# Sixteen attention chunks on TensorE: a planner's order, and an order that is written down

## The chip, the cores and the metric

The kernel runs on one core of a Trainium2 chip. The core has five engines that work side by side, each through its own queue and in the order of that queue: TensorE (PE) does matmuls, VectorE (DVE) and ScalarE (ACT) do element-wise work, GpSimd (POOL) does some more of it, and SyncE (SP) issues DMA transfers. Semaphores tell one engine that another is done. The metric is the time of one execution on the device in microseconds (us); lower is better.

## The reference

The program is a trunk of two layers on 1024 tokens of width 1024. The part that matters here is the first head group of the first layer: sliding-window attention over chunks of 64 tokens, eight query heads, two key heads, each of width 64, a window of the own chunk and the two before, and one learned "sink" logit for each head:

```python
scores = jnp.einsum('bnqhgd,bnkhd->bnhgqk', qc, kb).astype(jnp.float32) * (d ** -0.5)
m = jnp.maximum(jnp.max(scores, axis=-1, keepdims=True), sink_logit)
p = jnp.exp(scores - m)
denom = jnp.sum(p, axis=-1, keepdims=True) + jnp.exp(sink_logit - m)
p = (p / denom).astype(v.dtype)
out = jnp.einsum('bnhgqk,bnkhd->bnqhgd', p, vb)
```

Beside it the same layer has retention heads and gates, `y = concat(ya * silu(ag), yb * silu(bg)) @ w_out`, and every layer ends with a cross-attention into 256 memory tokens, whose keys are `memn @ wkv`. The second layer is a gated convolution.

## The kernel before

All activations lie transposed, width on the 128 partitions and tokens along the free dimension. Every fp32 operand is split into a high and a low part in a format with fewer bits, and a product is three matmuls, high-high, low-high and high-low (`mm3`, lines 210 to 216). `split` makes the two parts: ScalarE copies (line 230), VectorE subtracts (line 231).

A *projection* (`dense`, line 218) multiplies one weight tile of 128 output rows with all tokens: two halves of 512 tokens, each 8 x 3 = 24 matmuls of 512 columns, then a scaling by VectorE (`scaled`, line 303). A *key tile* (one step of `keys_out`, line 849) makes 128 rows of the memory's keys: 24 matmuls of 256 columns, a split, and two stores to DRAM. Its input is the normalised memory, which `mem_norm` has stored to DRAM and `mem_parts` loads back (line 845). The weights of both arrive through `Weights`: a raw tile is loaded by SyncE (line 86, two buffers), copied by ScalarE (line 97) and subtracted by VectorE (line 98) into one of three pages, in the fixed order in which they are used.

`even_layer` (line 522) first makes keys, values and queries of the window attention, then goes through sixteen chunks. One chunk (`window_chunk`, line 370) does, in this order:

- split its queries (line 382), twelve score matmuls into two PSUM buffers (line 391; they use 64 of the 128 rows, so that two run side by side);
- the softmax: maxima (VectorE, line 394), the shift (lines 397 and 398), exponentials with sums (ScalarE, lines 400 and 403), then VectorE's sum with the sink, reciprocal and scaling (lines 404 to 407) into one of two buffers, `Pe` for even and `Po` for odd chunks;
- eight transposes on TensorE (line 421; four in the first two chunks) and their split into `Th` and `Tl`;
- six values matmuls (three in the first two chunks), and two copies that put the result where the queries were (line 432).

Behind each chunk the loop of lines 548 to 553 traces one piece of other work: one of the six gates' projections (at chunks 1, 3, 6, 8, 11 and 13) or one of the eight key tiles (at chunks 0, 2, 4, 5, 7, 9, 10 and 12). Behind the loop stand the SiLU of the gates (line 555), the product with the attention's result (line 558) and the retention heads with their own projections.

The order in which the program is traced is not the order in which the engines run it. A planner walks through all instructions with estimated durations and appends to each engine's queue whatever is ready first, earlier traced work going ahead. Only where the program asks for it is the order fixed: `issue_after(ins)` makes every instruction that is traced inside the block, and that runs on the engine of `ins`, stand behind `ins` in the queue. In the loop before, nothing is asked for.

Of the kernel before, what the change touches and what calls it, by code (L numbers as in the profile page):

```python
# [22 lines left out]
P = 128  # L23
# [9 lines left out]
EVEN_GATES = (1, 3, 6, 8, 11, 13)  # L33
# [126 lines left out]
class Trunk:  # L160
# [209 lines left out]
    def window_chunk(self, n, Q, Kh, Kl, V, Pt):  # L370
        nc = self.nc
        nk = min(n + 1, 3) * CH
        k0 = max(n - 2, 0) * CH
        odd = n % 2
        p0 = 256 - nk if odd else 0
        cols = slice(p0, p0 + nk)
        Q = Q[n // 8][:, :, (n % 8) * CH : (n % 8) * CH + CH]
        Pn = Pt[odd]

        qh = self.buf("k", "qh", (P, 256), F32R)  # L380
        ql = self.buf("k", "ql", (P, 256), F32R)
        self.split(qh.rearrange("p (j t) -> p j t", j=4), ql.rearrange("p (j t) -> p j t", j=4), Q)
        mx, nm, sm, es = (self.small(k) for k in ("mx", "nm", "sm", "es"))
        sc = [self.ps("sc") for _ in range(2)]
        rows = (slice(0, 64), slice(64, P))
        keys = slice(k0, k0 + nk)
        for jp in range(2):
            j = slice(jp * P, jp * P + P)
            for i, (a, b) in enumerate(((qh, Kh), (qh, Kl), (ql, Kh))):
                for g, r in enumerate(rows):  # L390
                    nc.tensor.matmul(sc[g][:, jp * 256 : jp * 256 + nk], a[r, j], b[r, keys],  # L391
                                     start=i == 0, stop=i == 2)
        for g, ps in enumerate(sc):
            nc.vector.tensor_reduce(mx[:, 2 * g : 2 * g + 2],
                                    ps.rearrange("p (a b) -> p a b", a=2)[:, :, :nk],
                                    AX.X, ALU.max)
        nc.vector.scalar_tensor_tensor(nm, mx, -0.125, self.nsink, ALU.mult, ALU.min)
        nc.vector.tensor_tensor(es, self.sink, nm, op=ALU.add)
        for c in range(4):
            nc.scalar.activation(Pn[:, c, cols], sc[c // 2][:, (c % 2) * 256 : (c % 2) * 256 + nk],  # L400
                                 AF.Exp, bias=nm[:, c : c + 1], scale=0.125,
                                 accum_out=sm[:, c : c + 1])
        nc.scalar.activation(es, es, AF.Exp)
        nc.vector.tensor_tensor(sm, sm, es, op=ALU.add)
        nc.vector.reciprocal(sm, sm)
        for c in range(4):
            nc.vector.tensor_scalar(Pn[:, c, cols], Pn[:, c, cols], sm[:, c : c + 1], None,
                                    ALU.mult)
        Th = self.buf("T", "Th", (P, 2, H), F32R)
        Tl = self.buf("T", "Tl", (P, 2, H), F32R)  # L410
        if n == 0:
            kks = [(0, 0, 64)]
        elif n == 1:
            kks = [(1, 0, P)]
        else:
            b = (n - 3) // 2 if odd else (n - 2) // 2
            kks = [(0, b, P), (1, b + 1, P)]
        for kk, _, rows in kks:
            ps = self.ps("a")
            for c in range(4):  # L420
                nc.tensor.transpose(ps[:rows, c * P : c * P + P],  # L421
                                    Pn[:, c, kk * P : kk * P + rows], self.ident)
            self.split(Th[:rows, kk, :], Tl[:rows, kk, :], ps[:rows, :])
        ps = self.ps("a")
        for i, (kk, b, rows) in enumerate(kks):
            v = slice(b * P, b * P + P)
            self.mm3(ps, V[0][:rows, v], V[1][:rows, v], Th[:rows, kk, :], Tl[:rows, kk, :],
                     i == 0, i == len(kks) - 1)
        for g in range(2):
            r = slice(64 * g, 64 * g + 64)  # L430
            o = ps[r, g * 256 : g * 256 + 256].rearrange("p (j t) -> p j t", j=4)
            nc.vector.tensor_copy(Q[r], o)

    def to_tokens(self, vt, name):

        hi = self.buf("v", name + "h", dt=F32R)
        lo = self.buf("v", name + "l", dt=F32R)
        for h in range(2):
            ps = self.ps("a")
            for i in range(4):  # L440
                c = h * H + i * P
                self.nc.tensor.transpose(ps[:, i * P : i * P + P], vt[:, c : c + P], self.ident)
            c = slice(h * H, h * H + H)
            self.split(hi[:, c], lo[:, c], ps)
        return hi, lo
# [76 lines left out]
    def even_layer(self, xs):  # L522


        nc, io = self.nc, self.io
        k = self.buf("r", "ak")
        self.dense(xs, self.scaled(lambda a, b: k[:, a:b]), tags=("d", "d"))
        Kh, Kl = self.buf("v", "Kh", dt=F32R), self.buf("v", "Kl", dt=F32R)
# [3 lines left out]
        V = self.to_tokens(v, "V")  # L532
        Q = [self.buf("e", "Q", (P, 4, H)) for _ in range(2)]
# [4 lines left out]
        Pt = [self.buf("T", "Pe", (P, 4, 256)), self.buf("T", "Po", (P, 4, 256))]  # L538
# [4 lines left out]
        gates = [lambda a, b, j=j: G[a // H][:, j, :] for j in range(4)]  # L543
# [1 line left out]

        ya = self.dp.tile([2, P, 4, H], F32, name="ya")
        keys = self.keys_out(self.mem_parts(0, "r"), 0, "t")
        for n in range(16):
            self.window_chunk(n, Q, Kh, Kl, V, Pt)
            if n in EVEN_GATES:  # L550
                self.dense(xs, self.scaled(gates[EVEN_GATES.index(n)]))
            else:
                next(keys, None)
        for g in G + GB:
            nc.scalar.activation(g, g, AF.Silu)
        self.use_set(LN_EXP)
# [29 lines left out]
        V = next(kv)  # L586
# [560 lines left out]
```

## Time and profile before

| | us |
|---|---|
| timed runs, median of 3 | 1472.85 |
| lowest and highest run | 1469.6 and 3709.59 |
| profiled execution, its own time | 1468.65 |
| profiled execution, span of the trace | 1466.9 |
| TensorE busy in the span | 1437.5 |
| VectorE busy | 882.2 |
| ScalarE busy | 632.2 |

The granted clock of TensorE is 0.996 on the mean. Rows of the timeline give the start of an instruction, its duration and its engine, line, operands and shape. Matmuls overlap, so their durations are longer than the distance between their starts. Rows of groups give the count behind an x, then the busy time, the mean duration in ns and the idle time before. Rows of stretches give, for a stretch of time, the busy time and number of instructions of TensorE's matmuls, its weight loads, VectorE, ScalarE and GpSimd, then the granted clock, the DMA share and the GB/s.

### The profile page before, as it was taken

Reading aid. Unit: us, or ns where it says so; the run is one execution under the profiler, and the core shown is the slowest. Engines: PE = TensorE matmul, PEld = TensorE weight load, DVE = VectorE, ACT = ScalarE, POOL = GpSimd, SP = SyncE. Lnnn points to the kernel's source line nnn. Section 1 sums busy time; section 2 is a strip of 40 time slices with the busy share of each in tenths; the row PEclk is TensorE's granted clock in tenths of the full one; section 3 lists DMA queues with packets and bytes.
Section 4 is the critical chain, followed back from the end, with each engine's and each line's share of the span. In section 5 each row is a group of like instructions: output and inputs, shape, how many; then the busy total and the mean of one; then the engine's idle time right before and its main releaser. Section 6 shows DMA issues by size and latency. Waiting matters only on the chain.

```text
span 1466.9 us, 18556 instructions
## 1 busy us (share of the span) xinstructions
PE 1437.5 (98%) x7128; PEld 1210.0 (82%) x7128; DVE 882.2 (60%) x1317; ACT 632.2 (43%) x1140; POOL 258.5 (18%) x172
## 2 busy tenths in 40 slices
PE   7999999999998999999999999999999999999997
PEld 5888878888887888888887788888888888888996
DVE  7656767677755346447456986655566327446555
ACT  6434553344346234335334633333352325335554
POOL 2300102234211220000113034222220220000221
PEclk9999999999999999999999999999999999999999
DMA  6442223322354421113765121121135532111464
GB/s 218 148 168 58 90 70 101 101 72 59 112 214 152 155 101 44 30 29 126 223 207 180 47 85 60 58 58 58 58 109 192 187 129 72 37 36 39 128 216 149
DMA packets 55080, 160.45 MB, mean 109 GB/s; under 512 B 6736, under 2 KB 17104, under 8 KB 54224
## 3 DMA queue, kind: packets, MB, share of 16 engines
q1 hardware_dynamic: 54992, 159.27, 33.5%
q8 instruction: 56, 0.92, 0.3%
q14 instruction: 32, 0.26, 0.1%
HBM read 127.78 MB, written 27.26 MB: 106 GB/s over the span
## 4 chain that ended last, share of the span: by engine, by line
PE 86%; DVE 6%; DMA 3%; ACT 2%; issue 1%; SPq 0%; POOL 0%; DVEq 0%; ACTq 0%; POOLq 0%
PE psd L214 18%; PE psd L215 18%; PE psd L216 18%; PE pssc L215 5%; PE pssc L216 5%; PE pssc L214 5%; PE psa L215 4%; PE psa L214 4%; PE psa L216 4%; PE pssc L391 1%; DVE wlo L98 1%; DMA wraw<-w_o 1%; PE psa L421 1%; PE psa L931 1%; DMA wraw<-w_o_in 1%
## 5 line engine op out<-in xcount | busy, mean ns | idle before, releaser
L214 PE MATMUL psd<-xh,whi 128*128 128x512 f32 (+2 forms) x1096 | 412.7, 380 | 10.9 <-ACT whi L97 7.5
L215 PE MATMUL psd<-xl,whi 128*128 128x512 f32 (+2 forms) x1096 | 415.0, 380 | 0.0
L216 PE MATMUL psd<-xh,wlo 128*128 128x512 f32 (+2 forms) x1096 | 414.3, 379 | 0.3 <-DVE wlo L98 0.3
L214 PEld LDWEIGHTS psd<-xh,whi 128*128 128x128 f32 x1096 | 205.9, 188 | 48.3 <-ACT whi L97 8.0
L97 ACT CAST whi<-wraw 128x1024 fp32r<-128x1024 f32 (+1 forms) x136 | 141.8, 1045 | 219.5 <-PE psd L215 137.5
L216 PEld LDWEIGHTS psd<-xh,wlo 128*128 128x128 f32 x1096 | 206.1, 188 | 35.4 <-DVE wlo L98 0.6
L215 PEld LDWEIGHTS psd<-xl,whi 128*128 128x128 f32 x1096 | 206.2, 188 | 34.1 <-DVE xl L243 0.3
L98 DVE TENSOR_TENSOR wlo<-wraw,whi 128x1024 fp32r<-128x1024 f32 (+1 forms) x136 | 171.1, 1260 | 71.4 <-ACT whi L97 71.2
L274 POOL TENSOR_TENSOR ssq<-ssq,xold 128x512 f32<-128x512 f32 (+2 forms) x54 | 84.3, 1561 | 621.5 <-ACT xold L272 566.5
L316 DVE TENSOR_TENSOR xnew<-psd,xold 128x512 f32<-128x512 f32 x32 | 21.9, 690 | 97.6 <-PE psd L216 94.2
L126 ACT CAST wf<-ws 128x512 fp32r<-128x512 f32 x64 | 39.2, 621 | 90.4 <-PE pssc L216 27.2
L127 DVE TENSOR_TENSOR wf<-ws,wf 128x512 fp32r<-128x512 f32 x64 | 58.7, 922 | 23.0 <-ACT wf L126 22.6
L272 ACT ACTIVATE xold<-xnew 128x512 f32<-128x512 f32 (+2 forms) x63 | 36.5, 580 | 66.0 <-DVE xnew L316 33.8
L215 PE MATMUL pssc<-T,wf 128*128 128x512 f32 x156 | 61.3, 394 | 2.2 <-DVE T L231 2.2
L230 ACT CAST Th<-psa 128x512 fp32r<-128x512 f32 (+1 forms) x62 | 34.5, 590 | 64.3 <-PE psa L421 34.5
L214 PE MATMUL pssc<-T,wf 128*128 128x512 f32 x156 | 61.2, 393 | 0.8 <-ACT kept L738 0.8
L216 PE MATMUL pssc<-T,wf 128*128 128x512 f32 x156 | 61.0, 392 | 0.0
L231 DVE TENSOR_TENSOR Tl<-psa,Th 128x512 fp32r<-128x512 f32 (+1 forms) x62 | 41.7, 686 | 25.9 <-ACT Th L230 25.8
L109 POOL TENSOR_TENSOR ws<-wraw 128x512 f32<-128x512 f32 x14 | 18.6, 1332 | 205.3 <-DMA wraw<-w_o_in 205.3
L303 DVE TENSOR_TENSOR q<-psd,R 128x512 f32<-128x512 f32 x32 | 22.1, 691 | 53.8 <-PE psd L216 53.8
L214 PE MATMUL psd<-y,whi 128*128 128x512 f32 x128 | 50.0, 391 | 0.0
L215 PE MATMUL psd<-y,whi 128*128 128x512 f32 x128 | 50.0, 391 | 0.0
(339 smaller groups left out, 2888.1 us busy)
## 6 DMA issues: line engine op xcount, KB each, us to landing
wraw<-w_o SPq DMA_DIRECT2D x40, 512.0 KB, 3.7
wraw<-w_o_in SPq DMA_DIRECT2D x37, 512.0 KB, 3.5
wraw<-w_e_in SPq DMA_DIRECT2D x25, 512.0 KB, 3.8
wraw<-w_k SPq DMA_DIRECT2D x16, 512.0 KB, 4.0
mn<-memn SPq DMA_DIRECT2D x16, 512.0 KB, 4.8
wraw<-w_v SPq DMA_DIRECT2D x16, 512.0 KB, 4.5
xold<-x SPq DMA_DIRECT2D x16, 512.0 KB, 4.9
x<-xnew SPq DMA_DIRECT2D x16, 512.0 KB, 2.6
```

The lines of the kernel that those rows point to most:

```text
L97: self.nc.scalar.copy(hi[:, c], raw[:, c])
L98: self.nc.vector.tensor_tensor(lo[:, c], raw[:, c], hi[:, c].bitcast(F32), op=ALU.subtract)
L126: self.nc.scalar.copy(hi, src)
L127: self.nc.vector.tensor_tensor(lo, src, hi.bitcast(F32), op=ALU.subtract)
L214: mm(o, ah, bh, start=first, stop=False, skip_group_check=more)
L215: mm(o, ah, bl, start=False, stop=False, skip_group_check=more)
L216: self.last_mm = mm(o, al, bh, start=False, stop=last, skip_group_check=more)
L230: self.last_cast = self.nc.scalar.copy(hi, src)
L231: return (eng or self.nc.vector).tensor_tensor(lo, src, hi.bitcast(F32), op=ALU.subtract)
L272: nc.scalar.activation(sq, x, AF.Square)
L274: eng.tensor_tensor(self.ssq[:, a:b], self.ssq[:, a:b], sq, op=ALU.add)
L303: return lambda a, b, ps: self.nc.vector.tensor_tensor(out(a, b), ps, self.R[:, a:b], op=ALU.mult)
```

## The change

`window_chunk` becomes a generator with three steps: queries, scores and softmax; transposes and their split; values and their copies. The function `step` runs the next step of a chunk inside `issue_after(self.last_mm.ins)`, so that its matmuls stand behind the last matmul of what was traced before; the gates and key tiles are traced inside such a block, too. `last_mm` is now also set by scores and transposes. The loop traces, for each n from 0 to 16: the gate or key tile of n, the values of chunk n - 1, the scores of chunk n + 1, and the transposes of chunk n. TensorE's order from the first scores to the last values is thereby one row; the order within the other engines remains the planner's, and so does the place of all that is traced behind the loop.

```diff
@@ window_chunk
-                    nc.tensor.matmul(sc[g][:, jp * 256 : jp * 256 + nk], a[r, j], b[r, keys],
-                                     start=i == 0, stop=i == 2)
+                    self.last_mm = nc.tensor.matmul(
+                        sc[g][:, jp * 256 : jp * 256 + nk], a[r, j], b[r, keys],
+                        start=i == 0, stop=i == 2)
...
+        yield
         Th = self.buf("T", "Th", (P, 2, H), F32R)
...
-                nc.tensor.transpose(ps[:rows, c * P : c * P + P],
-                                    Pn[:, c, kk * P : kk * P + rows], self.ident)
+                self.last_mm = nc.tensor.transpose(ps[:rows, c * P : c * P + P],
+                                                   Pn[:, c, kk * P : kk * P + rows], self.ident)
             self.split(Th[:rows, kk, :], Tl[:rows, kk, :], ps[:rows, :])
+        yield
...
             nc.vector.tensor_copy(Q[r], o)
+        yield
@@ even_layer
-        for n in range(16):
-            self.window_chunk(n, Q, Kh, Kl, V, Pt)
-            if n in EVEN_GATES:
-                self.dense(xs, self.scaled(gates[EVEN_GATES.index(n)]))
-            else:
-                next(keys, None)
+        chunks = [self.window_chunk(n, Q, Kh, Kl, V, Pt) for n in range(16)]
+
+        def step(n):
+
+            if 0 <= n < 16:
+                with self.tc.issue_after(self.last_mm.ins):
+                    next(chunks[n])
+
+        step(0)
+        for n in range(17):
+            with self.tc.issue_after(self.last_mm.ins):
+                if n in EVEN_GATES:
+                    self.dense(xs, self.scaled(gates[EVEN_GATES.index(n)]))
+                elif n < 16:
+                    next(keys, None)
+            step(n - 1)
+            step(n + 1)
+            step(n)
```

## The prediction

> **What bounds the kernel now.** I read the page first, then the stretch table cut to the window stage, then the groups of that stage by shape, then the timeline of TensorE and of the two vector engines.
>
> ```profile
> PE 1437.5 (98%) x7128; PEld 1210.0 (82%) x7128; DVE 882.2 (60%) x1317; ACT 632.2 (43%) x1140; POOL 258.5 (18%) x172
> ```
>
> TensorE (PE) is busy for 98% of the span, so time can only be won by making its instructions follow each other faster, and any wait that is put in front of it is lost at once. The stage that the change touches runs from the first scores at 80 us to the last values at 249 us:
>
> ```profile
> 80.00:249.00 169.00, 169.00 (x977) 138.26 (x976) 111.90 (x277) 80.95 (x223) 7.00 (x2) 1.00 0.28 86
> ```
>
> In 169.0 us TensorE does 977 matmuls and is never idle; VectorE (DVE) is busy 111.9 us, ScalarE (ACT) 81.0. So there is no wait here that the change could remove. What it can remove is slowness inside the busy time. The groups say what the 977 are:
>
> ```profile
> L215 PE MATMUL psd<-xl,whi 128*128 128x512 f32 x128 | 50.5, 394 | 0.0
> L215 PE MATMUL psd<-mn,whi 128*128 128x256 f32 x64 | 18.4, 288 | 0.0
> L215 PE MATMUL psa<-Tl,Vh 128*128 128x512 f32 x29 | 11.9, 410 | 0.0
> L391 PE MATMUL pssc<-Kl,qh 64*128 64x192 f32 x56 | 11.6, 287 | 0.0
> L421 PE MATMUL psa<-ident,Po 128*128 128x128 f32 x60 | 8.7, 278 | 0.0
> L98 DVE TENSOR_TENSOR wlo<-wraw,whi 128x1024 fp32r<-128x1024 f32 x16 | 19.5, 1221 | 4.4 <-ACT whi L97 4.4
> ```
>
> Each product is three matmuls (L214 to L216), and the first chunk has smaller shapes under rows of their own. So: 192 matmuls for key tiles, 90 for values, 192 scores (three kinds of 64), 120 transposes (60 of odd chunks, as many of even ones), and the remaining 383 are projections: 288 of the six gates and 95 of the retention's first projections, which the planner has already pulled forward into this stage.
>
> **What TensorE pays for changing its kind of work.** Durations of overlapping matmuls mislead; the distance from start to start is what a matmul costs.
>
> ```profile
> 128.95 0.39 PE L216 MATMUL psd<-xh,wlo 128*128 128x512 f32 x1
> 129.27 0.37 PE L391 MATMUL pssc<-Kh,qh 64*128 64x192 f32 x2
> ...
> 130.13 0.50 PE L214 MATMUL psd<-xh,whi 128*128 128x512 f32 x1
> 130.46 0.40 PE L215 MATMUL psd<-xl,whi 128*128 128x512 f32 x1
> ...
> 130.93 0.40 PE L214 MATMUL psd<-xh,whi 128*128 128x512 f32 x1
> 131.16 1.04 PE L421 MATMUL psa<-ident,Pe 128*128 128x128 f32 x8
> 131.96 0.48 PE L215 MATMUL psd<-xl,whi 128*128 128x512 f32 x1
> 132.27 0.39 PE L216 MATMUL psd<-xh,wlo 128*128 128x512 f32 x1
> ...
> 134.99 0.39 PE L216 MATMUL psd<-xh,wlo 128*128 128x512 f32 x1
> ```
>
> A 512-column matmul behind its like costs 0.227 us (132.27 to 134.99 are twelve of them). The step into scores, which use half of the rows, costs 0.32 (128.95 to 129.27), 0.09 more; all twelve scores of a chunk cost 0.86 (129.27 to 130.13); the first matmul behind them costs 0.33, another 0.10. Eight transposes between projections cost 0.80, 0.10 each. Where scores are cut up, each piece pays again:
>
> ```profile
> 138.68 0.50 PE L214 MATMUL psa<-Th,Vh 128*128 128x512 f32 x1
> 139.11 0.35 PE L391 MATMUL pssc<-Kh,qh 64*128 64x192 f32 x1
> ```
>
> ```profile
> 110.21 1.09 PE L421 MATMUL psa<-ident,Pe 128*128 128x128 f32 x8
> 111.23 0.35 PE L391 MATMUL pssc<-Kl,qh 64*128 64x192 f32 x1
> ```
>
> One values matmul between two pieces of scores takes 0.43 instead of 0.23, and eight transposes that are put into the middle of a score block take 1.02 instead of 0.80.
>
> **The change, part by part.** It removes and adds no instruction that computes, and its edges stand between instructions of one engine, so they bring no semaphore either. *First*, the scores become whole. Priced by the starts above, with 0.120 us for a 256-column matmul:
>
> ```profile
> 122.09 0.28 PE L214 MATMUL psd<-mn,whi 128*128 128x256 f32 x1
> 122.21 0.28 PE L215 MATMUL psd<-mn,whi 128*128 128x256 f32 x1
> ```
>
> 383 x 0.227 + 192 x 0.120 + 90 x 0.227 + 120 x 0.10 + 16 x (0.09 + 0.86 + 0.10) = 86.9 + 23.0 + 20.4 + 12.0 + 16.8 = 159.2 us. The stage takes 169.0, so 9.8 us go. If transposes that follow scores cost 1.02 in the new order too, 15 x 0.22 = 3.3 less goes, 6.5; if the step from scores to transposes pays no 0.10, 1.6 more, 11.4. I take 9.8, since the new order has a projection or key tile behind the transposes, as in the 0.80 case.
>
> *Second*, the freedom to fill waits goes. Now the planner cuts gates and key tiles into pieces and lays them wherever chunk work is not ready. Afterwards everything on TensorE from chunk 0 to chunk 15 stands in one row: filler n, values n-1, scores n+1, transposes n. If transposes n wait, the next whole filler, the next values and scores stand behind them, and only later projections, which are outside the chain, may slip between; these have their weights late, in the last three or four steps. So the price is: how long does softmax n take, from its scores to its normalised rows, against what TensorE has to do meanwhile? Its work in between is transposes n-1, the filler, values n-1 and scores n+1: 0.80 + filler + 6 x 0.227 + 0.95. With a gate as filler (48 x 0.227 = 10.9) this is 14.0 us, with a key tile (24 x 0.120 = 2.9) 6.0. The softmax of chunk 8, whose scores are through when the matmul of 158.63 starts:
>
> ```profile
> 158.63 0.50 PE L214 MATMUL psd<-xh,whi 128*128 128x512 f32 x1
> ```
>
> ```profile
> 158.78 1.02 DVE L394 TENSOR_REDUCE mx<-pssc 128x2 f32<-128x384 f32 x2
> ...
> 161.80 0.68 DVE L231 TENSOR_TENSOR Tl<-psa,Th 128x512 fp32r<-128x512 f32 x1
> ...
> 163.65 1.01 DVE L407 TENSOR_SCALAR Pe<-Pe,sm 128x192 f32<-128x192 f32 x4
> ```
>
> It ends at 163.65 + 1.01 = 164.66, that is 6.0 us after its scores, with the splits of the previous chunk's transposes (Tl) in between, as they will be afterwards. Gates cover that with 8 us to spare. Key tiles cover it with nothing to spare, in eight places (n = 0, 2, 4, 5, 7, 9, 10, 12). A late one is chunk 9, where ScalarE had been sent to the SiLU of the gates and had to reload its table before the exponentials:
>
> ```profile
> 170.93 0.39 PE L214 MATMUL psd<-mn,whi 128*128 128x256 f32 x1
> ```
>
> ```profile
> 175.06 1.28 ACT L400 ACT_TABLE_LOAD   x1 [3.73 <-DVE nm L397]
> ```
>
> ```profile
> 180.40 0.32 DVE L407 TENSOR_SCALAR Po<-Po,sm 128x192 f32<-128x192 f32 x1
> ```
>
> 180.72 - 170.93 = 9.8 us. So one wait costs between 0 and 3.8 us. VectorE has 111.9 / 16 = 7.0 us of work for each chunk, a little less beside a key tile, which has no gate to scale; against 6.0 of TensorE it falls behind by about 1 us where two key tiles follow each other. I take 0.5 us for a lone key tile (n = 2, 4, 7), 1.0 for the second of a pair (5, 10), 2.0 at n = 9 (the table reload of 1.28 and a SiLU in front of it, half hidden under gate 8) and 1.5 at n = 12 (the same for the smaller SiLU): 1.5 + 2.0 + 2.0 + 1.5 = 7.0. Steps 14 and 15 have no key tile left; there the retention's projections fill, as they do now.
>
> *Third*, key tile 0 must be whole before gate 0. Its second half waits for the normalised memory that comes back from DRAM:
>
> ```profile
> L845 SPq DMA_DIRECT2D mn<-memn x4: 320/320/378, 63.5 to 77.7; - x4
> ...
> DMA to landing us min/median/max: 4.2/6.2/7.0
> ```
>
> The last load goes out at 77.7 and lands at 83.9 by the median. Scores 0 and half a key tile take TensorE to 80.4 + 0.9 + 1.4 = 82.7. Now gate 0 covers the rest; afterwards 1.2 us are a wait (0 to 2.0 by the shortest and longest landing).
>
> *At no cost*: the weights. A raw tile and its split (L98, 1.22 us, and as much again for ScalarE's copy) start when the tile three before is done, so even a pair of key steps gives them 12 us. SyncE's queue keeps its loads and the stores of the keys in the same sequence; its DMA share is 0.28. Nothing on GpSimd is moved; its two instructions are 7.0 us. Were a weight late all the same, it would be a wait like those above.
>
> Sum: 1468.65 (the profiled execution) - 9.8 + 7.0 + 1.2 = 1467.0. The timed runs of before lie 1 to 4 us above that execution, so I say 1468. Own range: saving 6.5 to 11.4, waits half to twice as long, and the 1 us of the timed runs: 1462 to 1480.
>
> **The rivals.** *The softmax is in time* (chance 0.25): only the 1.2 us of key tile 0 are left: 1460, timed 1461. For it: VectorE idles 57 us of the stage, and the order of its work is planned anew. Against: 6.0 against 6.0 leaves no room.
>
> *The softmax is late at every key tile* (0.17): as late as chunk 9, eight times 3.8 = 30 us against the 9.8, 1489. For it: fixed order with nothing to lay in between, weight splits of 1.22 us that come free just when a filler ends. Against: only that chunk met a table reload. From 4.9 us for each key tile (29.4 + 9.8, over 8) it is slower than before by 2%.
>
> *Such waits also slow the clock* (0.05). The trace has one place of that kind:
>
> ```profile
> 460.00:464.00 4.00, 1.28 (x6) 0.86 (x5) 1.77 (x2) 1.04 (x1) 1.88 (x1) 1.00 0.44 131
> 464.00:468.00 4.00, 4.00 (x12) 3.13 (x11) 0.21 (x1) 0.11 (x1) 0.00 (x0) 0.57 0.00 0
> ```
>
> After 2.7 us idle out of 4 the clock was 0.57 for the next 4 us, 1.7 us lost. With waits of 3.8 at eight key tiles that is 14 us more: 1503. Waits of 0.5 to 2 us, as in my sum, are shorter than that idle time, and I charge them nothing. [...]
>
> *The order hardly changes* (0.05), because planner and chain agree already: 1469. The rows at 138.68 and 110.21 speak against it.
>
> **How the numbers follow.** Forecast 0.46, rivals as above, 0.02 for a gain that I don't see. From 1455 to 1490 lies all but the clock's rival, the worst part of the late one and the unseen gain, 0.14 together. Two per cent, 29 us, is about what a measurement here tells from no change. The whole switching cost is 11.4 at most, so faster by that has 0.02; slower needs the clock's rival or the end of the late one: 0.07; within: 0.91.
>
> **What would show it.** After: score stretches of twelve, each behind values and followed by eight transposes; their starts 0.9 and 0.8 apart. TensorE idle in the stage of about 8 us, in front of transposes, ended by the normalise of L407, at key steps only, and one of 1.2 ended by a memory load. Clock 1.00 throughout. I am wrong if idle time stands in front of scores or values, if a wait is above 3 us, or if the stages behind differ by more than 5 us.

## The result, and the profile after

The changed kernel takes 1491.1 us (median of four runs, 1488.9 to 1496.9) against 1472.2 for the kernel before on the same chip: a ratio of 1.013, with an interval of 1.0105 to 1.0156. It is slower, by less than 2%. One run of the kernel before took 3710 us; the ratio leaves it out. The profiled execution took 1491.64 us, its span is 1489.9 us, 23.0 more than before, and the mean granted clock is 0.986 (before 0.996). In the changed file the scores are L391, the exponentials L401, the scalings L408, the transposes L423, and the product with the attention's result L574.

The engine row of the page after:

```profile
PE 1445.6 (97%) x7128; PEld 1221.1 (82%) x7128; DVE 871.1 (58%) x1317; ACT 632.3 (42%) x1140; POOL 255.6 (17%) x172
```

TensorE does the same 7128 matmuls in 8.1 us more of busy time, and the rest of the 23 us is idle time. To see where, I cut both traces at the same work: first scores, last values, first matmul of the second half's memory values, last matmul. Stretch rows of before, then of after (columns as before: busy time and count of matmuls, weight loads, VectorE, ScalarE, GpSimd, then clock, DMA share, GB/s):

```profile
80.40:248.50 168.10, 168.10 (x972) 137.71 (x972) 111.53 (x276) 80.54 (x222) 7.00 (x2) 1.00 0.28 85
248.50:423.20 174.70, 174.49 (x865) 146.90 (x864) 124.34 (x153) 65.88 (x119) 60.22 (x36) 1.00 0.33 103
423.20:1456.50 1033.30, 1022.04 (x4987) 868.04 (x4986) 588.18 (x810) 442.39 (x739) 170.21 (x115) 1.00 0.33 107
```

```profile
80.10:257.40 177.30, 169.44 (x957) 143.02 (x957) 109.07 (x273) 80.73 (x222) 5.66 (x2) 0.94 0.26 77
257.40:442.80 185.40, 178.29 (x882) 149.73 (x882) 118.04 (x155) 65.15 (x119) 59.74 (x37) 1.00 0.33 101
442.80:1479.50 1036.70, 1024.66 (x4986) 870.34 (x4985) 585.62 (x810) 443.12 (x739) 169.10 (x115) 0.99 0.33 106
```

The counts differ because the planner now pulls 16 projection matmuls fewer into the stage (363 instead of 379); at 0.227 us that is 3.6 us of work moved from the first row to the second. With that put right, the window stage lost 177.3 - 168.1 + 3.6 = 12.8 us, the stage behind it 185.4 - 174.7 - 3.6 = 7.1, all the rest 3.4. Most of the new clock loss lies in the first row (0.94), the new idle time in the first (7.9) and in the second (7.1, before 0.2).

**The waits in the stage.** Groups of after on TensorE between 80 and 258 us; the last part is the idle time before them and what ended it:

```profile
L391 PE MATMUL pssc<-Kh,qh 64*128 64x192 f32 x56 | 13.1, 323 | 1.5 <-ACT Pe L401 1.1 <-ACT Po L401 0.5
L215 PE MATMUL psa<-Tl,Vh 128*128 128x512 f32 x29 | 12.2, 421 | 2.2 <-DVE Tl L231 2.2
L423 PE MATMUL psa<-ident,Po 128*128 128x128 f32 x60 | 10.0, 318 | 1.5 <-DVE Po L408 1.5
L423 PE MATMUL psa<-ident,Pe 128*128 128x128 f32 x56 | 8.1, 290 | 2.6 <-DVE Pe L408 2.6
```

They sum to 7.8 us. About half (4.1) stands in front of transposes and is ended by the scaling L408. The rest stands in front of scores, ended by the exponentials that still read the score buffers, and in front of one values step, ended by a split.

**The order, and the clock behind a wait.** TensorE's timeline of after around chunk 5, where two key tiles follow each other, and a chunk without a wait:

```profile
132.58 0.35 PE L391 MATMUL pssc<-Kh,qh 64*128 64x192 f32 x1 [0.49 <-ACT Po L401]
132.77 0.27 PE L391 MATMUL pssc<-Kl,qh 64*128 64x192 f32 x1
...
134.03 0.27 PE L391 MATMUL pssc<-Kh,ql 64*128 64x192 f32 x1
135.78 1.94 PE L423 MATMUL psa<-ident,Po 128*128 128x128 f32 x8 [1.48 <-DVE Po L408]
137.37 0.78 PE L214 MATMUL psd<-xh,whi 128*128 128x512 f32 x1
137.94 0.63 PE L215 MATMUL psd<-xl,whi 128*128 128x512 f32 x1
138.37 0.63 PE L216 MATMUL psd<-xh,wlo 128*128 128x512 f32 x1
...
151.89 0.36 PE L391 MATMUL pssc<-Kh,qh 64*128 64x192 f32 x2
...
152.53 0.27 PE L391 MATMUL pssc<-Kh,ql 64*128 64x192 f32 x2
152.74 0.66 PE L423 MATMUL psa<-ident,Pe 128*128 128x128 f32 x4
```

Three things are to be seen. The order is as written: twelve scores, eight transposes, then a gate (the last row counts four transposes, since the window of that view ends inside them). At 151.89 the scores stand as x2, the two halves of the rows side by side, and the transposes start 0.85 us after the first score; at 132.58 they stand as x1, one after the other, and from the first start to the last takes 1.45 us instead of 0.64. And behind the two waits of 0.49 and 1.48 us a 512-column matmul takes 0.43 us from start to start (137.94 to 138.37) instead of 0.227. The stretch rows of after show how long that lasts:

```profile
134.00:142.00 8.00, 6.52 (x22) 5.42 (x22) 4.94 (x19) 3.30 (x12) 0.00 (x0) 0.57 0.20 75
142.00:179.00 37.00, 35.51 (x213) 29.96 (x212) 22.02 (x43) 16.21 (x34) 4.59 (x1) 1.00 0.18 50
179.00:190.00 11.00, 10.26 (x45) 9.15 (x46) 7.87 (x22) 5.79 (x15) 0.00 (x0) 0.53 0.47 164
190.00:196.00 6.00, 3.85 (x25) 3.00 (x23) 4.21 (x12) 3.69 (x13) 0.00 (x0) 1.00 0.41 106
196.00:200.00 4.00, 3.96 (x15) 3.43 (x16) 2.91 (x12) 2.54 (x11) 0.00 (x0) 0.57 0.13 47
```

Three spells at half clock, each with waits of 0.5 to 2.2 us at or just before its start: 8 x 0.43 + 11 x 0.47 + 4 x 0.43 = 10.3 us of clock lost, some of it in time that was idle anyway. The wait of 1.10 us in front of the transposes of chunk 2, at 105.96, has no such spell behind it in this trace.

**The long wait, and GpSimd.** Timelines of GpSimd, VectorE and TensorE of after around chunk 8:

```profile
174.10 1.02 DVE L395 TENSOR_REDUCE mx<-pssc 128x2 f32<-128x384 f32 x2
...
174.22 4.59 POOL L574 TENSOR_TENSOR GA<-GA,Q 128x2048 f32<-128x2048 f32 x1 [98.74 <-ACT qh L230]
...
175.04 4.04 DVE L231 TENSOR_TENSOR ql<-Q,qh 128x256 fp32r<-128x256 f32 x1
...
177.12 0.39 PE L214 MATMUL psa<-Th,Vh 128*128 128x512 f32 x1
...
179.01 0.68 DVE L231 TENSOR_TENSOR Tl<-psa,Th 128x512 fp32r<-128x512 f32 x1
...
179.74 0.80 PE L215 MATMUL psa<-Tl,Vh 128*128 128x512 f32 x1 [2.23 <-DVE Tl L231]
```

The first half of the gates' product runs on GpSimd for 4.59 us. The split `ql` on VectorE, 0.4 us elsewhere, runs beside it for 4.04 and ends when it ends; the splits `Tl` queue behind it, and the values step waits 2.23 us. Before, the same product met `ql` only in its last part: `ql` took 1.80 us, and TensorE did not wait. The second half of the product has a collision of its own, behind the stage:

```profile
262.45 4.62 POOL L574 TENSOR_TENSOR GA<-GA,Q 128x2048 f32<-128x2048 f32 x1 [3.73 <-DVE Q L435]
...
262.65 5.51 DVE L231 TENSOR_TENSOR rot<-bk,rot 128x1024 fp32r<-128x1024 f32 x1 [0.34 <-ACT rot L230]
268.19 0.69 DVE L303 TENSOR_TENSOR bq<-psd,R 128x512 f32<-128x512 f32 x1
...
268.91 0.47 SPq L456 DMA_DIRECT2D swap<-bq  x1
...
275.61 0.66 PE L446 MATMUL psa<-ident,bv 128*128 128x128 f32 x4 [1.65 <-DVE bv L303]
279.58 0.68 PE L214 MATMUL pssc<-rot,rot 128*128 128x512 f32 x2 [2.15 <-ACT rot L230]
```

The retention's rotation split takes 5.51 us instead of 1.23, the scaling of `bq` stands behind it until 268.19, so the DMA that swaps its halves goes out at 268.91, and TensorE waits 1.65 and 2.15 us for what follows from that; a wait of 3.28 us at 327.56 comes later in the same stage. Before, this product stretched the same split (to 4.95 us), but the scaling of `bq` ran ahead of it, at 250.08, and TensorE waited for nothing.

### The profile page after: what moved, and what is told of

It is laid out like the page before. It is cut to its first block, busy times and chain, and to the rows that moved or that the text cites. A ratio compares the mean times of both kernels' runs of the same rounds, so it can differ in the third digit from the quotient of the medians.

```text
span 1489.9 us, 18557 instructions
## 1 busy us (share of the span) xinstructions
PE 1445.6 (97%) x7128; PEld 1221.1 (82%) x7128; DVE 871.1 (58%) x1317; ACT 632.3 (42%) x1140; POOL 255.6 (17%) x172
## 4 chain that ended last, share of the span: by engine, by line
PE 84%; DVE 6%; DMA 4%; ACT 2%; issue 1%; POOL 1%; SPq 0%; DVEq 0%; ACTq 0%; POOLq 0%
PE psd L214 17%; PE psd L215 17%; PE psd L216 17%; PE pssc L215 6%; PE pssc L216 5%; PE pssc L214 5%; PE psa L215 4%; PE psa L214 4%; PE psa L216 4%; DVE wlo L98 1%; PE psa L423 1%; DMA wraw<-w_o 1%; PE psa L947 1%; PE pssc L391 1%; DMA wraw<-w_o_in 1%
## 5 line engine op out<-in xcount | busy, mean ns | idle before, releaser
L98 DVE TENSOR_TENSOR wlo<-wraw,whi 128x1024 fp32r<-128x1024 f32 (+1 forms) x136 | 167.4, 1233 | 76.4 <-ACT whi L97 75.8
```

Source lines behind the costliest of these rows:

```text
L98: self.nc.vector.tensor_tensor(lo[:, c], raw[:, c], hi[:, c].bitcast(F32), op=ALU.subtract)
```

## The experiments

**The product on VectorE.** If the collision is the cause of the 2.23 us and of the waits behind the stage, the product's engine decides, with the written order untouched.

```diff
-            nc.gpsimd.tensor_tensor(G[h], G[h], Q[h], op=ALU.mult)
+            nc.vector.tensor_tensor(G[h], G[h], Q[h], op=ALU.mult)
```

> The changed kernel with one edit: the product of gate and attention result (two instructions of 128x2048) goes from GpSimd to VectorE. Theory A (GpSimd's 4.6 us product slows VectorE beside it: 4.04 us instead of 0.41 for the split of the queries behind chunk 9's maxima, 5.51 instead of 1.22 for the rotated keys later): the wait of 2.2 us before values 8, the clock of 0.66 behind it (some 5 us) and the two waits at 275 to 280 us (3.8 us) go, against 1491 about 1480. Theory B (the softmax's own length against a key tile is the cause, GpSimd is by the way): within 3 us of 1491. Theory C (VectorE's 2 x 2.4 us more lie in the softmax's way): 1491 or more, with new waits before transposes.

Measured: 1484.9 us, 1.0094 of before (1.0071 to 1.0117). Its stretches, stage and behind:

```profile
81.50:255.00 173.50, 166.07 (x958) 140.38 (x957) 107.83 (x274) 81.07 (x222) 1.15 (x1) 0.95 0.26 79
255.00:434.70 179.70, 178.87 (x882) 149.79 (x881) 127.41 (x156) 65.57 (x119) 57.50 (x36) 1.00 0.33 104
```

Behind the stage 5.7 of the 7.1 us are back (185.4 to 179.7). In the stage 3.8 us are back: the values step waits 0.80 instead of 2.23, since the product takes 2.28 us of VectorE itself, and idle time and half clock remain (0.95). So the collision is part of the cause: most of the loss behind the stage, but the smaller part of the loss in it.

**The same in the kernel before**, as a control: if GpSimd's product were simply a bad choice, moving it would make the kernel before faster, too.

```diff
 # in the kernel before
-            nc.gpsimd.tensor_tensor(G[h], G[h], Q[h], op=ALU.mult)
+            nc.vector.tensor_tensor(G[h], G[h], Q[h], op=ALU.mult)
```

> Control: the kernel before, with the product on VectorE. TensorE has no idle time there that the product could have caused, so within 2 us of the kernel before. If it gains 5 us or more, the product was a cost before, too, and what it cost the changed kernel was not brought by the change.

Measured: 1474.5 us, 1.0018 (1.0009 to 1.0028). In the old order the product on GpSimd costs nothing, so what it costs in the new order comes from the change.

**Only the second half of the product**, to part the two collisions.

```diff
-            nc.gpsimd.tensor_tensor(G[h], G[h], Q[h], op=ALU.mult)
+            (nc.vector if h else nc.gpsimd).tensor_tensor(G[h], G[h], Q[h], op=ALU.mult)
```

> The changed kernel with only the second of the two products (behind the last chunk) on VectorE; the first stays on GpSimd beside chunk 9. Theory A, in its two places: the wait of 2.2 us before values 8 and the clock behind it stay, the waits of 1.6, 2.2 and 3.3 us behind the stage go: 1491 less 5 to 6, 1485. If the later waits come from the projections being later: 1490 or more.

Measured: 1487.2 us, 1.0111 (1.0094 to 1.0128). The two rows that matter, the stretch behind the stage and the values step of chunk 8:

```profile
257.60:437.20 179.60, 178.84 (x882) 149.80 (x881) 125.48 (x156) 65.59 (x119) 58.51 (x36) 1.00 0.33 104
```

```profile
180.66 0.50 PE L215 MATMUL psa<-Tl,Vh 128*128 128x512 f32 x1 [2.23 <-DVE Tl L231]
```

The stage behind is repaired by this half alone (5.8 us of span), the 2.23 us in the stage stay. Each half of the product has its own price, as its rows said. The span is 5.1 us shorter than that of the kernel after, the median 3.9; by the timed runs alone the two are not told apart (1.0111 and 1.013, with intervals that overlap), so this rests on the rows.

**No two key tiles in a row.** If VectorE falls behind where two key tiles follow each other, spreading the gates evenly takes those waits away.

```diff
-EVEN_GATES = (1, 3, 6, 8, 11, 13)
+EVEN_GATES = (1, 3, 5, 7, 9, 11)
```

> The changed kernel with the gates at chunks 1, 3, 5, 7, 9 and 11, so that no key tile follows a key tile before chunk 13. Theory B: the waits of 0.5 and 1.5 us at chunk 5 and of 0.7 and 1.5 us at chunk 10, and the half clock behind them (3.3 and 2 us), go; some 8 us less, 1483. The wait at GpSimd's product moves from chunk 9 to the key step behind gate 7 and stays. If a lone key tile is as bad as a pair: within 3 us of 1491.

Measured: 1479.7 us, 1.0051 (1.0033 to 1.0069). Of the stage's waits over 0.4 us one is left, the 1.10 us in front of the transposes of chunk 2, and the stage takes 170.7 us with 32 projection matmuls more than after, 163.4 for the same work. The wait at GpSimd's product, which I expected to stay, is gone as well: `ql` is stretched here too, to 3.44 us, but a gate stands on TensorE beside it. So this edit takes away more than the pairs. And the one wait that is left, which left the clock at 1.00 in the kernel after, is followed by half clock here. Stretches of this experiment:

```profile
104.00:108.00 4.00, 2.90 (x16) 2.76 (x16) 3.91 (x12) 1.73 (x4) 0.00 (x0) 0.64 0.21 70
108.00:112.00 4.00, 4.00 (x11) 3.04 (x11) 2.66 (x10) 2.56 (x11) 0.00 (x0) 0.51 0.46 131
```

and of the kernel after, with the same wait:

```profile
104.00:108.00 4.00, 2.90 (x20) 2.59 (x20) 3.90 (x13) 2.47 (x5) 0.00 (x0) 1.00 0.21 70
```

**Spread gates and the product on VectorE.** The whole written order is kept, both causes are taken away.

```diff
-EVEN_GATES = (1, 3, 6, 8, 11, 13)
+EVEN_GATES = (1, 3, 5, 7, 9, 11)
...
-            nc.gpsimd.tensor_tensor(G[h], G[h], Q[h], op=ALU.mult)
+            nc.vector.tensor_tensor(G[h], G[h], Q[h], op=ALU.mult)
```

> The changed kernel, its chain whole, with both causes taken out in other ways: gates at chunks 1, 3, 5, 7, 9 and 11, and the product on VectorE. If pairs of key tiles and the product are all that is wrong with it: 1491 less 11 (the pairs, as measured alone) less 5 to 6 (the product), 1474 to 1475, still no faster than before; the rest is the wait before transposes 2 and what the key steps lack. If the two overlap: 1479, as without pairs alone.

Measured: 1469.9 us, 0.9986 (0.9974 to 0.9999), better than I expected: the 1.1-us wait was there at 106.4 us, but this time the clock stayed at 1.00. So the written order need not be slow; what made the change slow was what it met. Whether the order itself is worth something this does not show: the interval ends just below 1, the gates stand at other chunks than in the kernel before, and the kernel before was not run with those places.

**The fillers free.** The chunks' steps stay in one row, but gates and key tiles are outside it and may be laid in anywhere, as before.

```diff
-            with self.tc.issue_after(self.last_mm.ins):
-                if n in EVEN_GATES:
-                    self.dense(xs, self.scaled(gates[EVEN_GATES.index(n)]))
-                elif n < 16:
-                    next(keys, None)
+            last = self.last_mm
+            if n in EVEN_GATES:
+                self.dense(xs, self.scaled(gates[EVEN_GATES.index(n)]))
+            elif n < 16:
+                next(keys, None)
+            self.last_mm = last
```

> The changed kernel with gates and key tiles out of the chain: the steps of the chunks stand behind each other as before the edit, but a gate or key tile may go anywhere among them, in pieces. Theory D (what costs is that no filler may go to where the chunk waits; the whole scores, transposes and values are a gain of some 10 us): no idle TensorE and no half clock in the stage, 1460 to 1465. Rival (the pieces of the fillers bring the switching back): 1470 to 1474, as the kernel before. Rival (whole chunk blocks are the cost): 1485 or more.

Measured: 1476.1 us, 1.0031 (1.0017 to 1.0046). The stage came out nearly as expected, at full clock and with 1.98 us of idle time left (1.41 in front of a values step, 0.57 in front of scores); the total didn't:

```profile
80.80:240.20 159.40, 157.42 (x956) 132.64 (x956) 108.99 (x273) 80.67 (x222) 5.67 (x2) 1.00 0.29 86
```

It does the work of the kernel after in 17.9 us less, at full clock. What I had missed is that the collision behind the stage is there again, with waits of 1.64, 2.16 and 3.2 us at 258, 262 and 310 us.

**Fillers free and the product on VectorE**, the two together:

```diff
-            with self.tc.issue_after(self.last_mm.ins):
-                if n in EVEN_GATES:
...
+            last = self.last_mm
+            if n in EVEN_GATES:
...
-            nc.gpsimd.tensor_tensor(G[h], G[h], Q[h], op=ALU.mult)
+            nc.vector.tensor_tensor(G[h], G[h], Q[h], op=ALU.mult)
```

> Both edits on the changed kernel: fillers out of the chain, and the product on VectorE. If the two losses are separate (fillers held back: the stage; GpSimd's product: chunk 9 and the rotations behind the stage), the stage stays as with free fillers alone, 159 us, or 2 less, and the waits of 7.0 us behind it go: 1476 less 7 to 9, 1467 to 1469, some 4 us faster than the kernel before. If the waits behind the stage come from the projections being done later, not from the product: 1474 or more.

Measured: 1467.6 us, 0.9966 (0.9952 to 0.9980), faster than both kernels by a little.

```profile
80.70:237.80 157.10, 157.10 (x956) 132.36 (x956) 107.89 (x274) 80.62 (x222) 1.10 (x1) 1.00 0.29 87
237.80:417.40 179.60, 178.89 (x882) 149.83 (x882) 125.55 (x156) 65.56 (x119) 58.65 (x36) 1.00 0.33 104
```

This is the change without its waits: no idle time in the stage, clock 1.00, the same 363 projections. The kernel before would take 168.1 - 3.6 = 164.5 us for this work, so the saving in switching is 7.4 us. **With spread gates as well**, on top of this edit:

```diff
-EVEN_GATES = (1, 3, 6, 8, 11, 13)
+EVEN_GATES = (1, 3, 5, 7, 9, 11)
```

> Free fillers and the product on VectorE as before, with the gates at chunks 1, 3, 5, 7, 9 and 11 too. With free fillers no wait is left in the stage, so the place of the gates should be worth nothing: 1466 to 1469. If pairs still cost something that the fillers' pieces only hide: 1462 to 1465.

Measured: 1466.6 us, 0.9971 (0.9959 to 0.9984): the same. Where the fillers are free, it doesn't matter at which chunk they are traced.

**Without the scalings.** Which of the stage's waits are VectorE's time for the end of the softmax?

```diff
-        nc.vector.tensor_tensor(sm, sm, es, op=ALU.add)
-        nc.vector.reciprocal(sm, sm)
-        for c in range(4):
-            nc.vector.tensor_scalar(Pn[:, c, cols], Pn[:, c, cols], sm[:, c : c + 1], None,
-                                    ALU.mult)
```

> The changed kernel without the end of the softmax: the sum with the sink, the reciprocal and the four scalings of each chunk are left out (the exponentials go to the transposes unscaled), which takes some 1.6 us out of the softmax's length and of VectorE's work for each chunk. Theory B: the waits before transposes 2, 5, 10 and 12 and the half clock behind them go, the one at GpSimd's product stays: 1478 to 1483. Theory A alone: 1489 or more.

Measured: 1488.7 us, 1.012 (1.0101 to 1.0139). The stage gave back 8.3 us (169.0), and no transposes wait any more; 2.23 us in front of the values step and 0.7 to 0.9 in front of scores are left. The total missed my expectation. The waits behind the stage are other ones but sum to the same 7.1 us (3.86 and 3.23), and the clock, which had stayed at 1.00 behind them in the kernel after, was 0.57 from 270 to 274 us and from 321 to 325 us; that stretch is 2.4 us longer than after, and the first scores come 1.2 us later. I had counted neither, and the scalings have nothing to do with the collision there.

**Busy while it waits.** The half clock was so far only seen beside the waits. To measure its own price I left TensorE's order and what it waits for as they are, and put matmuls whose results are thrown away in front of the waiting steps, so that the array is busy while it would wait.

```diff
+            for _ in range(6 if n in (2, 5, 10) and kk == 0 else 0):
+                nc.tensor.matmul(ps, Kh[:, :P], Kh[:, :H], start=True, stop=True)
...
+        for _ in range(9 if n == 8 else 0):
+            nc.tensor.matmul(ps, Kh[:, :P], Kh[:, :H], start=True, stop=True)
```

> The changed kernel, its order untouched, with idle matmuls in four of its waits: six 512-column matmuls (1.4 us) in front of the transposes of chunks 2, 5 and 10, and nine (2.0 us) in front of the values of chunk 8; they write into the PSUM tile that the next instructions overwrite. Theory E (what the waits cost is mostly the half clock that follows them, 10.2 us in the stage, and TensorE at work keeps the clock up): the waits end at the same times, the clock stays at 1.00 and 6 to 10 us go, 1481 to 1485. Theory F (the clock falls for another reason, or the waits themselves are the cost): 1490 to 1494, since the matmuls only fill time or make the waits longer.

Measured: 1489.5 us, 1.0121 (1.0104 to 1.0137), no gain in the total. Stretches of the stage, then of two waits behind it:

```profile
80.80:251.80 171.00, 168.58 (x985) 141.75 (x985) 109.25 (x273) 80.67 (x222) 5.80 (x2) 0.99 0.27 79
275.00:280.00 5.00, 5.00 (x19) 4.14 (x18) 4.41 (x6) 2.76 (x6) 1.28 (x1) 0.66 0.14 27
325.00:330.00 5.00, 5.00 (x25) 4.11 (x25) 4.71 (x8) 3.81 (x9) 1.70 (x1) 0.86 0.01 3
```

The stage is 6.3 us shorter (171.0 against 177.3) although it does the 27 idle matmuls as well, and the clock is 0.99 instead of 0.94: as the half-clock theory says. But behind it the waits of 1.46 and 2.16 us, which had left the clock at 1.00 in the kernel after, now came with 0.66 in the 5 us after them, and the one of 3.2 us with 0.86. From 439.7 us on, in work that no edit touches, it also took 4.4 us longer than the kernel after, with a wait of 3.52 us at 827.11 where that has 1.90. Its profiled execution, 1492.96 us, is the highest of its runs. To keep that apart, the same **with the product on VectorE**, where nothing waits behind the stage; it is to be compared with the first experiment.

```diff
+            for _ in range(6 if n in (2, 5, 9) and kk == 0 else 0):
+                nc.tensor.matmul(ps, Kh[:, :P], Kh[:, :H], start=True, stop=True)
...
+        for _ in range(4 if n == 8 else 0):
+            nc.tensor.matmul(ps, Kh[:, :P], Kh[:, :H], start=True, stop=True)
...
-            nc.gpsimd.tensor_tensor(G[h], G[h], Q[h], op=ALU.mult)
+            nc.vector.tensor_tensor(G[h], G[h], Q[h], op=ALU.mult)
```

> The changed kernel with the product on VectorE (which has no wait behind the stage, 1.0094 of before) and idle matmuls in its waits: six in front of the transposes of chunks 2, 5 and 9, four in front of the values of chunk 8. Its stage had lost some 8.6 us to a clock below 1.00. Theory E: the clock stays at 1.00 in the stage, nothing behind it can take the gain back, 5 to 8 us less than with the product on VectorE alone: 1.004 to 1.006 of before, 1477 to 1480. Theory F: 1.009 of before or more, 1485.

Measured: 1478.5 us, 1.0036 (1.0024 to 1.0048), against 1.0094 for the first experiment; the two intervals don't touch.

```profile
81.90:248.70 166.80, 164.83 (x979) 138.35 (x979) 107.59 (x274) 80.88 (x222) 1.14 (x1) 1.00 0.27 82
```

The stage is 6.7 us shorter, the clock 1.00. Work that is thrown away makes the kernel 0.6% faster. VectorE, which sets the waits' ends, does the same work in both, and nothing but the clock and the idle time, which the idle matmuls fill, differs in the stage: the half clock behind short waits costs about 6.5 us. It is not the luck of one execution: the mean clock is 0.993 to 0.996 in all six runs, against 0.986 to 0.991 in the four of the first experiment.

## Why the prediction was wrong, point by point

**What bounds the kernel, and the saving: right, a little too large.** TensorE pays for switching, and whole scores save it: 7.4 us (fillers free, product on VectorE) where the step had 9.8 with a range of 6.5 to 11.4. The score blocks look as I said they would: 0.85 us from the first score to the transposes.

**A term that the saving lacked.** I priced all scores at 0.86 us, with both halves of the rows side by side. In the written order a score block often comes when the exponentials of the chunk before still hold the second score buffer. ScalarE's timeline of after:

```profile
132.32 0.20 ACT L401 ACTIVATION_READ_ACCUMULATOR Po<-pssc,nm 128x1 f32 x1
...
133.12 0.22 ACT L401 ACTIVATION_READ_ACCUMULATOR Po<-pssc,nm 128x1 f32 x1
```

These are the ends of the second and the fourth of four exponentials: the first two free the first buffer, at 132.52, the last two the second, at 133.34. The six scores of the first half go ahead (132.58), the other six follow, and nothing runs side by side: 1.45 us instead of 0.64. By the starts, eight of the sixteen blocks of after cost 5.2 us over 0.84 in this or a milder form, in the version with free fillers three, 1.4 us. That is 3.8 us of the saving lost again. I read this from the traces; no run tested it by itself.

**The waits: the sum right by luck, the places only in part.** The forecast was 7.0 for the softmax and 1.2 for the memory's load, 8.2; recorded are 7.8. That the sums agree is luck: 2.23 us of the 7.8 come from GpSimd's product, which the forecast had at nothing, 1.5 us stand in front of scores, and only 4.1 are of the kind that was forecast. It was right that key tiles in pairs are the worst: at n = 5 and n = 10 the step from scores to transposes waits 1.5 us, with 0.5 and 0.7 in front of the scores. It was wrong that a lone key tile costs 0.5 each (n = 4 and 7 cost nothing, n = 2 costs 1.4 by its two waits, of scores and of transposes), that n = 9 pays for the table reload (it paid 2.23 for GpSimd's product, and in front of values), that n = 12 costs 1.5 (it cost nothing), and that the memory's load costs 1.2: key tile 0 took 3.2 us instead of 2.9. Idle time in front of scores and values was named as a sign that I am wrong, and it came.

**The step that failed first** is "Waits of 0.5 to 2 us, as in my sum, are shorter than that idle time, and I charge them nothing". I had one place in the trace of before with low clock, behind 2.7 us of idle time in 4, and took its length for the condition. "The trace has one place of that kind" was a misreading: the same trace has a second one, behind two shorter waits. TensorE's timeline of before, and the stretch that follows:

```profile
836.26 0.49 PE L214 MATMUL pssc<-T,wf 128*128 128x512 f32 x1 [0.82 <-ACT kept L738]
838.73 0.50 PE L215 MATMUL pssc<-T,wf 128*128 128x512 f32 x1 [1.98 <-DVE T L231]
```

```profile
839.00:843.00 4.00, 4.00 (x12) 3.10 (x12) 4.00 (x8) 2.40 (x5) 0.00 (x0) 0.57 0.00 0
```

In the stage after, two waits of 0.49 and 1.48 us with scores between them were enough. The stage's account, against 164.5 for the same work before: - 7.4 saving, + 3.8 for scores that don't run side by side, + 7.8 idle, leaves 177.3 - 164.5 + 7.4 - 3.8 - 7.8 = 8.6 for the clock; the clock's rows lose 10.3, and the two runs with busy waits gave 6.3 and 6.7 of it back. By what is left over it is the largest term of the stage; by the two runs that tested it, it nearly eats up the saving. The rival "such waits also slow the clock" named the mechanism but asked for waits of 3.8 us. The runs give no length from which a wait halves the clock: in the stage after no idle time was longer than 2.23 us, the gap before 463.00 in the trace of before was 2.72 us, and the same 1.10-us wait left 1.00 in the kernel after and 0.64 and then 0.51 with spread gates. What they do show is how long a spell lasts: in the traces of before and after every spell of half clock between the first and the last matmul takes 3.4 us or two or three times that (in after, in the stage, 135.03 to 141.86, 179.40 to 189.64, 196.47 to 199.88).

**The step that failed second** is "Nothing on GpSimd is moved". Its two instructions were not, but what VectorE does beside them was: an earlier first half stretched `ql` from 1.80 to 4.04 us, and the rotation split that the second half holds up now stands ahead of the scaling of `bq`. That is 5.7 of the 7.1 us behind the stage (179.7 and 179.6 without it), and the 2.23 us in the stage. In the rows of after `ql`, with both inputs in SBUF, takes 4.04 us beside the product and ends 0.27 us after it; in the first experiment, without GpSimd's product beside it, it takes 0.42. The maxima, read from PSUM, take 1.02 us beside the product in after and 1.02 in the first experiment. What makes the two differ no run tested. "The stages behind differ by more than 5 us" was the sign for it, and so was a wait above 3 us (3.28).

**The rivals.** "The softmax is late at every key tile" has nearly the time that came, 1489, but not the reason: its waits would have been 30 us, there were 7.8. My sum was 1467.0 for the profiled execution, which took 1491.64: 24.6 too low. By its terms that is 2.4 for the smaller saving, 3.8 for the scores, 8.6 for the clock (what was left over, above, so the sum must close), 7.1 for the stage behind and 3.4 for the rest, less 0.4 for the waits and 0.3 for a stage that begins earlier: 24.6.

**Open.** The 3.4 us behind 442.8 us. The control has 2.9 of them without the written order (426.1 to its last matmul takes 1036.2), and in every experiment this stretch is 2.3 to 7.8 us longer than in the trace of before, so they look like a short profiled execution of before rather than like the change; the medians of the timed runs differ by 19.0 us, not by 23.0. By the clock's rows 3.4 us more are lost between 820 and 870 us after than before, but the waits there are the same ones (0.82 and 1.98 us, ending at 859.59 after). Open, too, is what decides whether a short wait is followed by half clock. And the last 1.4 us of the stage behind, which stay when the product is moved.

## What to carry to other kernels

Fix only that part of an order that pays, here the chunk's own steps, and leave the fillers free to go where a wait opens: that version, with the product of 4.6 us moved from GpSimd to VectorE, takes 0.9966 of the kernel before. Price a wait on TensorE with the clock behind it: here waits of 0.5 to 2.2 us came with half-clock spells of 3.4 to 10 us, and the same wait of 1.10 us passed without one in two traces of five. And where an order is planned anew, look at what now runs beside each long GpSimd instruction, also in stages that the change doesn't touch: here `ql` took 4.04 us instead of 0.42 beside one, and the rotation split 5.51 instead of 1.23.

## What the runs showed that I had not expected

The clock's answer to a wait depends on more than its length: 0.49 and 1.48 us, 1.7 us apart, halved it for 7 us, while 3.28 us left it at 1.00. Nor is the answer always the same. The 3.2-us wait of that step came with 3.4 us of half clock in three other traces (fillers free, without the scalings, the first one busy while it waits). The 1.10-us wait of chunk 2 stands in five traces: nothing followed it in two, 3.4 us of half clock in two, 6.8 us in one. And the two waits of 0.8 and 2.0 us that before has at 836 and 839 us came with 3.4 us of half clock in four traces (before, the control, only the second half of the product, fillers free with the product on VectorE), and with 6.8 us in that of after. A single profile therefore doesn't give the price of a wait; several runs do. Stretch of after, behind the wait that ends at 327.56:

```profile
326.00:328.00 2.00, 0.44 (x2) 0.40 (x3) 0.89 (x2) 1.54 (x2) 1.27 (x1) 1.00 0.00 0
328.00:330.00 2.00, 2.00 (x11) 1.70 (x10) 1.39 (x2) 1.94 (x6) 0.00 (x0) 1.00 0.00 0
```

And 22 matmuls whose results are thrown away, laid into such waits, made a kernel faster by 0.6% (1.0094 to 1.0036 of the kernel before).
